# Where the quads stand in a two-layer encoder: one fewer in layer A's output projection, three more in layer B

## The chip, the cores and the metric

The kernel runs on one core of one Trainium2 chip. A core has a matrix engine (TensorE, PE in the profile, with its weight loads as PEld), a vector engine (VectorE, DVE), a scalar engine (ScalarE, ACT), GpSimd (POOL) and a queue engine (SyncE, SP), each with its own instruction stream in a fixed order; semaphores tie the streams together. The metric is the device time of one execution in microseconds. Each version is timed in several runs, and one further execution is profiled.

## The reference

The input x has 256 rows (frames) of 2048 values, all in float32. Two layers and a last norm:

```python
# layer A (chunked attention, 32 heads of 128, chunks of 64 frames)
h = rms_norm(x, a_norm)
q, k, v, g = jnp.split(h @ a_w_in, 4, axis=-1)          # 2048 -> 4 x 4096
o = chunked_relbias_attention(q, k, v, a_rel_bias)
x = x + (o * silu(g)) @ a_w_out                          # 4096 -> 2048
# shared keys and values, and the forget gate
h_kv = rms_norm(x, kv_norm)
k_s, v_s = jnp.split(h_kv @ kv_w, 2, axis=-1)            # 2048 -> 2 x 4096
logf = log_sigmoid(h_kv @ f_w + f_b);  cum = cumsum(logf)
# layer B (forgetting attention: logits q.k/sqrt(128) + cum[t] - cum[s], causal)
q, g = jnp.split(rms_norm(x, b_norm) @ b_w_in, 2, axis=-1)   # 2048 -> 2 x 4096
o = forgetting_attention(q, k_s, v_s, cum)
x = x + (o * silu(g)) @ b_w_out                          # 4096 -> 2048
return rms_norm(x, final_norm)
```

Nearly all of the arithmetic is in the four projections, whose weights are read once.

## The kernel before, in words

**Products.** The weights stay float32 in memory. Each weight tile (`raw`) is split into a high part (`hi`, rounded, made by ScalarE, L243 or L248) and a low part (`lo`, the rest, made by VectorE, L244 or L249); the activations are split the same way once (`xT`, `oA`, `x1T`, `oB`, each with an h and an l). A product is three matmuls, high by high, low by high, high by low, of 128x128 against 128x512 (L185). A *unit* is 512 output columns for all 256 rows (two accumulators); an *entry* is a block of two k-rows (256 input features) of one unit: 2 x 2 x 3 = 12 matmuls. Splits are kept in four buffers each (`SPLIT`), raw tiles in six (`RAW`), so ScalarE and VectorE can run at most four entries ahead of TensorE.

**Quads.** For a pair of units, block b of both may be done together by Winograd's scheme with 7 instead of 8 block products (class `Quad`): 21 matmuls in place of 24. For it VectorE forms four sums of weights (L300, L301, L311, L312) and four low parts (L308), ScalarE the high parts (L306), and the left side needs sums of its own per block (`sum_up`, L393 to L401: five additions, a high part on ScalarE at L400, a low part at L401). Some of the seven products go into sums `p1`, `p5`, `p6`, `p7` that several quads share; after the last quad of a pair they are combined (L351 to L355) and added to what the units give (`add_combined`, L831, or `add_whole`).

**Stages.** Sixteen groups of two heads in layer A (`aqk`, `avg` units, two quads per pair from group 1 on), the output projection of layer A (units `ao0` to `ao3`, 16 entries each), sixteen groups in layer B (`bqg`, `bkv` units, one quad per pair from group 1 on), the output projection of layer B (`bo0` to `bo3`). The forget gate is worked out in group 0 of layer B, in pieces (`forget`, with `zp`, `fps`, the chain on `f_work`, `cp`, `cT`), one piece at a time between the entries of `bkv0` as `FORGET_STEPS` says.

**The attention of a group** is a generator whose steps are woven between the projection's entries. Its steps: split the turned q and k (`wide`, `q`); the scores (`s1p`, `s0p`, L552 and L576) and the softmax; the weights and the gate are turned (`turn`): VectorE transposes in 32x32 blocks (`sgY`, L522), and sixteen transfers, eight each from GpSimd and SP, carry the blocks to their places (`sgZ`, L525); split the turned weights (`wide`, L544 on ScalarE and L545 on VectorE); the product with v (`op`, L552 to L554 and L616); and the gated result goes into the next projection's left side (`oT`, L620, then `oAh`/`oAl` or `oBh`/`oBl`). The output projection therefore needs its last k-rows (entry 15) only after the last attention.

**Order.** `project` (L482) runs an output projection through a list of entries and quads, `Quads.order` makes it: `lead` entries, a quad, three entries, a quad, and so on. After each item the side generators advance by a table of counts: `[4, 1, 0, 1, 5, 1, 1]` means the first step after the fourth item, the next after one more, and so on. The sums of the quads (`open`) have such a table too. The splits are issued four entries ahead. On each engine the instructions run in the order in which the program issues them.

## Time and profile before

| | |
|---|---|
| median of 3 runs | 1736.14 us (1734.17 to 1737.35) |
| profiled execution | 1732.83 us, its span 1731.1 us |
| TensorE busy | 1710.2 us, 99% of the span |
| VectorE busy | 1561.4 us, 90% |
| ScalarE busy | 1195.1 us, 69% |
| GpSimd busy | 301.0 us, 17% |
| DMA, mean | 229 GB/s |

Layer A's groups run to about 690 us, its output projection to about 862, layer B's groups to about 1560, and its output projection to the end. In lines of the profile a number behind L is the line of the kernel before, names are those of the program without buffer numbers, `x` gives the count, a pair of numbers in front of a timeline's row is start and duration, and the brackets at its end give the idle time of the engine before it and what ended it. A matmul's duration is that of its passage through a pipeline; the distance of two starts is what it costs.

### The profile page before, as it was taken

The numbers are of one execution on the slowest core, as the hardware profiler recorded it, in microseconds if no ns is written. First come the engines' busy times: TensorE is split into PE (matmuls) and PEld (weight loads), VectorE is DVE, ScalarE is ACT, GpSimd is POOL, SyncE is SP. The second block draws the span as 40 slices with busy tenths as digits, with TensorE's granted clock in tenths as the row PEclk, the third lists the DMA queues.
The fourth block names the chain that finished last, engine by engine and source line by source line (L and its number), as shares of the span: only waits on it lengthen the run. The fifth ranks groups of instructions, "written<-read, shape, count | busy, mean of one in ns | idle before, by whom it ended". The sixth has DMA issues, their size and how long they took to land.

```text
span 1731.1 us, 26983 instructions
## 1 busy us (share of the span) xinstructions
PE 1710.2 (99%) x8213; PEld 1498.4 (87%) x8213; DVE 1561.4 (90%) x2378; ACT 1195.1 (69%) x2115; POOL 301.0 (17%) x623
## 2 busy tenths in 40 slices
PE   9999999999999999899999999999999999999997
PEld 7888888888888888788888888888888888888886
DVE  8799998999999999888978999999999989996887
ACT  7666666666666666555658788778788878775554
POOL 1011111111111111103102222222222222221000
PEclk9999999999999999999999999999999999999999
DMA  8666666776666666566766666666666666667654
GB/s 309 210 228 245 232 233 206 237 240 235 233 225 231 228 237 231 196 232 225 269 217 219 222 234 231 225 232 229 227 231 232 226 226 229 251 233 251 221 195 146
DMA packets 150320, 396.44 MB, mean 229 GB/s; under 512 B 31104, under 2 KB 51872, under 8 KB 150048
## 3 DMA queue, kind: packets, MB, share of 16 engines
q1 hardware_dynamic: 131536, 373.16, 61.7%
q0 software_dynamic: 17920, 20.48, 4.5%
q8 instruction: 66, 1.08, 0.3%
q10 hardware_dynamic: 720, 1.07, 0.2%
q14 instruction: 78, 0.64, 0.1%
HBM read 351.05 MB, written 4.23 MB: 205 GB/s over the span
## 4 chain that ended last, share of the span: by engine, by line
PE 93%; DVE 3%; DMA 1%; ACT 1%; issue 1%; POOL 0%; SPq 0%; ACTq 0%; DVEq 0%
PE bkv_acc L185 17%; PE bqg_acc L185 17%; PE avg_acc L185 14%; PE aqk_acc L185 13%; PE bo_acc L185 8%; PE ao_acc L185 6%; PE p L553 3%; PE p L554 3%; PE p L552 3%; PE op L616 1%; PE aqk_acc L553 1%; PE s0p L576 1%; PE aqk_acc L554 1%; PE aqk_acc L552 1%; DVE quad_lo L308 1%
## 5 line engine op out<-in xcount | busy, mean ns | idle before, releaser
L525 POOL DMA_DIRECT2D sums<-first x256 | 126.1, 500 | 549.8 <-DVE oT L620 262.5
L243 ACT ACTIVATE bqg_hi<-bqg_raw,gain 128x512 fp32r<-128x512 f32 x226 | 149.5, 713 | 85.6 <-issue 24.9
L244 DVE SCALAR_TENSOR_TENSOR bkv_lo<-bkv_raw,gain,bkv_hi 128x512 fp32r<-128x512 f32 x226 | 161.3, 760 | 17.1 <-ACT bkv_hi L243 16.8
L185 PE MATMUL bkv_acc<-bkv_hi,x1Th 128*128 128x512 f32 x452 | 167.5, 382 | 0.0
L185 PE MATMUL bqg_acc<-bqg_hi,x1Th 128*128 128x512 f32 x452 | 167.4, 382 | 0.0
L185 PE MATMUL bqg_acc<-bqg_lo,x1Th 128*128 128x512 f32 x452 | 166.1, 379 | 0.0
L185 PE MATMUL bkv_acc<-bkv_hi,x1Tl 128*128 128x512 f32 x452 | 166.1, 379 | 0.0
L185 PE MATMUL bkv_acc<-bkv_lo,x1Th 128*128 128x512 f32 x452 | 166.1, 379 | 0.0
L185 PE MATMUL bqg_acc<-bqg_hi,x1Tl 128*128 128x512 f32 x452 | 166.1, 379 | 0.0
L243 ACT ACTIVATE bkv_hi<-bkv_raw,gain 128x512 fp32r<-128x512 f32 x226 | 145.1, 711 | 22.4 <-issue 16.0
L244 DVE SCALAR_TENSOR_TENSOR bqg_lo<-bqg_raw,gain,bqg_hi 128x512 fp32r<-128x512 f32 x226 | 156.2, 741 | 4.6 <-ACT bqg_hi L243 4.5
L525 POOL DMA_DIRECT2D sgZ<-sgY x256 | 125.7, 499 | 156.2 <-PE avg_acc L185 66.7
L185 PE MATMUL aqk_acc<-aqk_hi,xTh 128*128 128x512 f32 x392 | 146.5, 387 | 0.1
L185 PE MATMUL aqk_acc<-aqk_lo,xTh 128*128 128x512 f32 x392 | 143.7, 380 | 1.1 <-DVE aqk_lo L249 1.0
L185 PE MATMUL avg_acc<-avg_hi,xTh 128*128 128x512 f32 x392 | 143.4, 379 | 0.0
L185 PE MATMUL avg_acc<-avg_hi,xTl 128*128 128x512 f32 x392 | 143.4, 379 | 0.0
L185 PE MATMUL avg_acc<-avg_lo,xTh 128*128 128x512 f32 x392 | 143.3, 379 | 0.0
L185 PE MATMUL aqk_acc<-aqk_hi,xTl 128*128 128x512 f32 x392 | 143.3, 379 | 0.0
L249 DVE TENSOR_TENSOR avg_lo<-avg_raw,avg_hi 128x1024 fp32r<-128x1024 f32 x97 | 116.1, 1222 | 16.5 <-ACT avg_hi L248 15.8
L248 ACT ACTIVATE aqk_hi<-aqk_raw 128x1024 fp32r<-128x1024 f32 x95 | 99.9, 1052 | 41.1 <-PE avg_acc L185 15.3
L248 ACT ACTIVATE avg_hi<-avg_raw 128x1024 fp32r<-128x1024 f32 x97 | 100.6, 1052 | 30.8 <-issue 18.1
L249 DVE TENSOR_TENSOR aqk_lo<-aqk_raw,aqk_hi 128x1024 fp32r<-128x1024 f32 x95 | 114.2, 1215 | 5.6 <-ACT aqk_hi L248 5.6
(373 smaller groups left out, 4595.8 us busy)
## 6 DMA issues: line engine op xcount, KB each, us to landing
bqg_raw<-in_b_w_in SPq DMA_DIRECT2D x128, 512.0 KB, 5.1
bkv_raw<-in_kv_w SPq DMA_DIRECT2D x128, 512.0 KB, 4.8
avg_raw<-in_a_w_in SPq DMA_DIRECT2D x127, 512.0 KB, 4.3
aqk_raw<-in_a_w_in SPq DMA_DIRECT2D x125, 512.0 KB, 5.3
ao_raw<-in_a_w_out SPq DMA_DIRECT2D x64, 512.0 KB, 4.7
bo_raw<-in_b_w_out SPq DMA_DIRECT2D x64, 512.0 KB, 4.4
sgZ<-sgY SPq DMA_DIRECT2D x256, 40.0 KB, 2.1
sgZ<-sgY POOLq DMA_DIRECT2D x256, 40.0 KB, 1.9
```

The lines of the kernel that those rows point to most:

```text
L185: pe.matmul(acc[t], x[:, t * P:(t + 1) * P], w, start=t not in begun, stop=last and i == 2)
L243: self.by_act = act.activation(hi[:, j], raw[:, j], AF.Copy, scale=gk)
L244: self.by_dve = dve.scalar_tensor_tensor(lo[:, j], raw[:, j], gk, r32(hi[:, j]), op0=OP.mult, op1=OP.subtract)
L248: self.by_act = act.activation(hi[:, j], raw[:, j], AF.Copy)
L249: self.by_dve = dve.tensor_sub(lo[:, j], raw[:, j], r32(hi[:, j]))
L308: feed.by_dve = dve.tensor_sub(lo[:, :n], src, r32(hi[:, :n]))
L525: queues[j].dma_start(out=r32(z)[j * SQ:(j + 1) * SQ, i], in_=y[i * SQ:(i + 1) * SQ, j])
L552: pe.matmul(out_, a[0], b[0], start=start, stop=False)
L553: pe.matmul(out_, a[0], b[1], start=False, stop=False)
L554: pe.matmul(out_, a[1], b[0], start=False, stop=stop)
L576: pe.matmul(s0p[:, i], q0[:, i], qkT[:, HG + i, 0], start=True, stop=True)
L616: pe.matmul(op[:, i, 1::NT], v1[:, i * DH:(i + 1) * DH], pT[:, i, NT], start=False, stop=i == HG - 1)
```

## The change

It moves quads and steps. Three things:

1. In layer A's output projection the first pair (`ao0`, `ao1`) has two quads instead of three, behind 17 entries instead of 14. The sums of its quads are opened after 8, 11, 30, 34 and 39 items instead of 3, 4, 5, 7 and 33. The steps of the last layer-A attention come one entry later each.
2. Group 0 of layer B has a quad for block 7, as the other groups have: `bqg0` and `bkv0` run seven blocks and a quad stands behind the third entry of `bkv0`. The sums of block 7 are made earlier (`sums_b`), and the pieces of the forget gate stand after entries 0, 1, 4 and 5 of `bkv0` instead of 0, 2, 6 and 7.
3. In layer B's output projection the first pair (`bo0`, `bo1`), which had plain entries alone, has two quads behind 17 entries. The sums are opened after 6, 10, 30, 34 and 39 items instead of 20, 22, 24, 26 and 28. In the last layer-B attention `wide` is split one item sooner (after 15), and `op` and `oT` come two items sooner (after 16 and 17).

In all the program has six matmuls fewer (7991 against 7997 rows on TensorE, 2049 against 2016 on VectorE). Lines of the changed kernel lie three to five lower.

```diff
--- before.py
+++ after.py
@@ -52,7 +52,7 @@
 TERMS = 8
 QUADS = 5
 HEAT = 9
-WAIT = 8
+WAIT = 5
 
 QUADS_A = (1, 2)
 QUADS_B = (2,)
@@ -61,7 +61,7 @@
 B1_STEPS = {3: 1, 5: 1, 6: 2}
 B2_STEPS = {1: 1}
 OLD_B_STEPS = {0: 1, 2: 99}
-FORGET_STEPS = {0: 1, 2: 1, 6: 1, 7: 1}
+FORGET_STEPS = {0: 1, 1: 1, 4: 1, 5: 1}
 
 
 def r32(ap):
@@ -360,10 +360,10 @@
         def __init__(self, name):
             self.name, self.sums = name, {}
 
-        def order(self, first, second, n, lead):
+        def order(self, first, second, n, lead, wait=3):
 
             a, b = ([(sp_, i) for i in range(n, sp_["nk"] // KB)] for sp_ in (first, second))
-            normal = a[:-1] + b[:3] + a[-1:] + b[3:]
+            normal = a[:-1] + b[:wait] + a[-1:] + b[wait:]
             out = normal[:lead]
             for i in range(n):
                 out.append((None, Quad(self, (first, second), i, not i, i == n - 1)))
@@ -430,17 +430,14 @@
     a_pairs = [paired(qkvg[2 * g:2 * g + 2], QUADS_A) for g in range(1, NG)]
     ao = [spec(f"ao{u}", a_w_out[u], KI) for u in range(4)]
     ao_quads, bo_quads = Quads("ao"), Quads("bo")
-    ao_order = ao_quads.order(ao[0], ao[1], 3, 14) + ao_quads.order(ao[2], ao[3], QUADS, 4)
+    ao_order = ao_quads.order(ao[0], ao[1], 2, 17) + ao_quads.order(ao[2], ao[3], QUADS, 4)
     todo += ao_order
     for g in range(NG):
-        qkvg.append(spec(f"bqg{g}", b_w_in[g], KD, g0=GB, quads=len(QUADS_B) * (g > 0)))
-        qkvg.append(spec(f"bkv{g}", kv_w[g], KD, g0=GKV, quads=len(QUADS_B) * (g > 0)))
+        qkvg.append(spec(f"bqg{g}", b_w_in[g], KD, g0=GB, quads=len(QUADS_B)))
+        qkvg.append(spec(f"bkv{g}", kv_w[g], KD, g0=GKV, quads=len(QUADS_B)))
     bo = [spec(f"bo{u}", b_w_out[u], KI, LATE if u == 3 else 0, KEPT if u == 3 else 0) for u in range(4)]
-    todo += whole(qkvg[2 * NG]) + whole(qkvg[2 * NG + 1])
-    b_pairs = [paired(qkvg[2 * g:2 * g + 2], QUADS_B) for g in range(NG + 1, 2 * NG)]
-    bo_order = whole(bo[0]) + whole(bo[1])
-    bo_order.insert(KI // KB + WAIT, bo_order.pop(KI // KB - 1))
-    bo_order += bo_quads.order(bo[2], bo[3], QUADS, 4)
+    b_pairs = [paired(qkvg[2 * g:2 * g + 2], QUADS_B) for g in range(NG, 2 * NG)]
+    bo_order = bo_quads.order(bo[0], bo[1], 2, 17, WAIT) + bo_quads.order(bo[2], bo[3], QUADS, 4)
     todo += bo_order
     feed = Feed(todo)
     order = iter(qkvg)
@@ -854,7 +851,7 @@
                            accum_out=ssq1[:, t, u:u + 1])
         return more and (more, [8, 7, 1, 1, 1] if u % 2 else [11, 1, 1, 1])
 
-    project(oA, ao, ao_order, ao_begun, ao_closed, [(prev, [4, 1, 0, 1, 5, 1, 1]), (ao_quads.open(oA, QUADS), [3, 1, 1, 2, 26])])
+    project(oA, ao, ao_order, ao_begun, ao_closed, [(prev, [5, 1, 0, 1, 5, 1, 1]), (ao_quads.open(oA, QUADS), [8, 3, 19, 4, 5])])
     tot1 = const.tile([P, NT], F32, name="tot1")
     dve.tensor_reduce(tot1, ssq1, axis=AX.X, op=OP.add)
     rsB, halfB = rstd_of(tot1, "b")
@@ -949,17 +946,13 @@
 
         qk, gs = accs["q"]
         kv = accs["kv"]
-        if g:
-            for t in range(NT):
-                whole_ = a_quads.comb[:, NT + t]
-                dve.scalar_tensor_tensor(qk[:, t, GC:], kv[t][:, :GC], rsB[:, t:t + 1], whole_[:, :GC],
-                                         op0=OP.mult, op1=OP.add)
-            for t in range(NT):
-                whole_ = a_quads.comb[:, NT + t]
-                dve.tensor_add(whole_[:, GC:], kv[t][:, GC:], whole_[:, GC:])
-            kv = [a_quads.comb[:, NT + t] for t in range(NT)]
-        else:
-            evac_scaled(kv, 0, GC, rsB, qk[:, :, GC:])
+        whole_ = [a_quads.comb[:, NT + t] for t in range(NT)]
+        for t in range(NT):
+            dve.scalar_tensor_tensor(qk[:, t, GC:], kv[t][:, :GC], rsB[:, t:t + 1], whole_[t][:, :GC],
+                                     op0=OP.mult, op1=OP.add)
+        for t in range(NT):
+            dve.tensor_add(whole_[t][:, GC:], kv[t][:, GC:], whole_[t][:, GC:])
+        kv = whole_
         rest_of = attention(g, biases, qk, lambda: (v, gs), halfB, oB, HALVES, ("last", "last"), home)
         next(rest_of)
         yield
@@ -967,8 +960,8 @@
         yield
         yield from rest_of
 
-    def open_b(accs, g):
-        qk, qg = rows(UN, "qk"), add_whole(accs["qg"], 0) if g else accs["qg"]
+    def open_b(accs):
+        qk, qg = rows(UN, "qk"), add_whole(accs["qg"], 0)
         evac_scaled(qg, 0, GC, rsB, qk[:, :, :GC])
         accs["q"] = qk, gate_from(qg, GC, halfB)
 
@@ -976,22 +969,24 @@
     fg = forget()
     for g in range(NG):
         accs = {}
+        first, second = (Unit(x1T, next(order)) for _ in range(2))
+
+        def sums_b():
+            finish(last[0])
+            a_quads.sum_up(x1T, KD // KB - 1, sums[:, 0], a_quads.comb)
+
+        def products():
+            b_pairs[g][0].step(x1T, first, second)
+            open_b(accs)
+            for t in range(NT):
+                k = a_quads.comb[:, NT + t, :GC]
+                act.activation(k, k, AF.Copy, scale=rsB[:, t:t + 1])
+
         if g:
-            first, second = (Unit(x1T, next(order)) for _ in range(2))
             accs["qg"] = drive(rest(first), prev, B1_STEPS, {}, old, OLD_B_STEPS)
-
-            def products():
-                b_pairs[g - 1][0].step(x1T, first, second)
-                open_b(accs, g)
-                for t in range(NT):
-                    k = a_quads.comb[:, NT + t, :GC]
-                    act.activation(k, k, AF.Copy, scale=rsB[:, t:t + 1])
-
-            accs["kv"] = drive(rest(second), prev, B2_STEPS, {QUADS_B[0]: products})
         else:
-            accs["qg"] = drive(unit(x1T), last[0], {2: 99})
-            accs["kv"] = drive(unit(x1T), fg, FORGET_STEPS, {2: lambda: open_b(accs, g)})
-            a_quads.sum_up(x1T, KD // KB - 1, sums[:, 0], a_quads.comb)
+            accs["qg"] = drive(rest(first), None, {}, {2: sums_b})
+        accs["kv"] = drive(rest(second), prev if g else fg, B2_STEPS if g else FORGET_STEPS, {QUADS_B[0]: products})
         old, prev = prev, side_b(g, accs)
         advance(prev)
 
@@ -1033,11 +1028,11 @@
     def bo_begun(u, left):
         if left == (4 if u else 1):
             load_xin(x1d, u)
-        if left == 2 and u == 3:
+        if left == 2 and u % 2:
             add_combined(bo_quads, u)
 
     def bo_closed(u, acc):
-        if u == 2:
+        if u % 2 == 0:
             add_combined(bo_quads, u)
         xin = xins.pop(u)
         for t in range(NT):
@@ -1047,8 +1042,8 @@
             if u == 3:
                 finish_tile(t)
 
-    project(oB, bo, bo_order, bo_begun, bo_closed, [(old, [1, 2, 0]), (prev, [4, 2, 1, 1, 1, 7, 2, 1]),
-                                                 (bo_quads.open(oB, QUADS), [20, 2, 2, 2, 2])])
+    project(oB, bo, bo_order, bo_begun, bo_closed, [(old, [1, 2, 0]), (prev, [4, 2, 1, 1, 1, 6, 1, 1]),
+                                                 (bo_quads.open(oB, QUADS), [6, 4, 20, 4, 5])])
 
 
 _INS = ["x", "x_t", "gains", "a_w_in", "a_rel_bias", "a_w_out", "kv_w", "f_w", "f_b", "b_w_in", "b_w_out",
```

Three places show what moves. In the rows, the number at the end of a name tells one buffer from another.

**VectorE in layer A's output projection, up to the transpose `sgY` of the last attention.** L249 is the low part of an entry, L393 to L401 are sums of a quad's left side, `csc` scales the softmax. Before:

```order
L396 TENSOR_TENSOR ao_quad_7189<-ao_quad_7189 128x128
L397 TENSOR_TENSOR ao_quad_7189<-ao_quad_7189 128x128
L398 TENSOR_TENSOR ao_quad_7189<-ao_quad_7189 128x128
L249 TENSOR_TENSOR ao0_lo12_7330<-ao0_raw12_7139,ao0_hi12_7329 128x1024
L399 TENSOR_TENSOR ao_quad_7189<-ao_quad_7189 128x128
L598 RECIPROCAL csc_7303<-sm_7265 128x4
L249 TENSOR_TENSOR ao0_lo13_7353<-ao0_raw13_7157,ao0_hi13_7352 128x1024
L401 TENSOR_TENSOR ao_sums2_7275<-ao_quad_7189,ao_sums2_7275 128x512
L599 TENSOR_TENSOR csc_7303<-csc_7303,half_a_395 128x4
L393 TENSOR_TENSOR ao_quad_7189<-oAh0_184,oAl0_188 128x512
L249 TENSOR_TENSOR ao0_lo14_7371<-ao0_raw14_7175,ao0_hi14_7370 128x1024
L522 STREAM_TRANSPOSE sgY_7310<-sg_7263 128x1280
```

The changed kernel, from the scores (`sg`) on:

```order
L586 SCALAR_TENSOR_TENSOR sg_7265<-s0p_7256,tb_7017 128x2x128
L587 TENSOR_REDUCE nm_7266<-sg_7265 128x2 x2
L249 TENSOR_TENSOR ao0_lo11_7278<-ao0_raw11_7139,ao0_hi11_7277 128x1024
L595 RECIPROCAL csc_7295<-sm_7267 128x4
L596 TENSOR_TENSOR csc_7295<-csc_7295,half_a_395 128x4
L249 TENSOR_TENSOR ao0_lo12_7322<-ao0_raw12_7157,ao0_hi12_7321 128x1024
L393 TENSOR_TENSOR ao_quad_7339<-oAh0_184,oAl0_188 128x512
L519 STREAM_TRANSPOSE sgY_7302<-sg_7265 128x1280
```

Of the sums that stood between the scores and the transpose one addition (L393) is left ahead of it; the rest now stands behind it.

**VectorE in layer B's output projection, from the transpose of the last attention to the split of `wide`.** Before:

```order
L249 TENSOR_TENSOR bo0_lo11_16429<-bo0_raw11_16270,bo0_hi11_16428 128x1024
L522 STREAM_TRANSPOSE sgY_16453<-sg_16398 128x1280
L249 TENSOR_TENSOR bo0_lo12_16473<-bo0_raw12_16302,bo0_hi12_16472 128x1024
L249 TENSOR_TENSOR bo0_lo13_16491<-bo0_raw13_16326,bo0_hi13_16490 128x1024
L249 TENSOR_TENSOR bo0_lo14_16509<-bo0_raw14_16344,bo0_hi14_16508 128x1024
L249 TENSOR_TENSOR bo1_lo0_16527<-bo1_raw0_16374,bo1_hi0_16526 128x1024
L249 TENSOR_TENSOR bo1_lo1_16545<-bo1_raw1_16410,bo1_hi1_16544 128x1024
L249 TENSOR_TENSOR bo1_lo2_16563<-bo1_raw2_16432,bo1_hi2_16562 128x1024
L249 TENSOR_TENSOR bo1_lo3_16585<-bo1_raw3_16476,bo1_hi3_16584 128x1024
L545 TENSOR_TENSOR wide_16602<-sgZ_16454,wide_16602 128x2x128 x2
```

The changed kernel, first around the transpose and then around `wide`:

```order
L249 TENSOR_TENSOR bo0_lo14_16499<-bo0_raw14_16317,bo0_hi14_16498 128x1024
L393 TENSOR_TENSOR bo_quad_16385<-oBh0_8665,oBl0_8669 128x512
L519 STREAM_TRANSPOSE sgY_16479<-sg_16422 128x1280
L396 TENSOR_TENSOR bo_quad_16385<-bo_quad_16385 128x128
L397 TENSOR_TENSOR bo_quad_16385<-bo_quad_16385 128x128
L398 TENSOR_TENSOR bo_quad_16385<-bo_quad_16385 128x128
L249 TENSOR_TENSOR bo1_lo2_16522<-bo1_raw2_16341,bo1_hi2_16521 128x1024
L399 TENSOR_TENSOR bo_quad_16385<-bo_quad_16385 128x128
```

```order
L249 TENSOR_TENSOR bo1_lo5_16578<-bo1_raw5_16434,bo1_hi5_16577 128x1024
L300 TENSOR_TENSOR bo_quad_16385<-bo1_raw0_16458,bo0_raw0_16456 128x512
L301 TENSOR_TENSOR bo_quad_16385<-bo1_raw0_16458 128x512
L308 TENSOR_TENSOR quad_lo0_16600<-bo0_raw0_16456,quad_hi0_16599 128x1024
L542 TENSOR_TENSOR wide_16617<-sgZ_16480,wide_16617 128x2x128
L311 TENSOR_TENSOR bo0_raw0_16456<-bo1_raw0_16458,bo_quad_16385 128x512
L542 TENSOR_TENSOR wide_16617<-sgZ_16480,wide_16617 128x2x128
L312 TENSOR_TENSOR bo0_raw0_16456<-bo0_raw0_16456 128x512
L308 TENSOR_TENSOR quad_lo1_16623<-bo_quad_16385,quad_hi1_16622 128x1024
```

The transpose has the thirteenth entry's low part and one addition ahead of it that stood behind it or were not there; `wide` stands two entries sooner, and the first sums and the first low part of a quad stand ahead of it.

**VectorE in group 0 of layer B, at the forget gate.** L894 to L910 before (L891 to L907 after) are the gate's chain, L244 the low part of an entry, L308 that of a quad. Before:

```order
L894 COPY f_work_8962<-fps_8959 128x64
L895 TENSOR_TENSOR f_work_8962<-f_work_8962,fps_8959 128x64
L244 SCALAR_TENSOR_TENSOR bkv0_lo6_8994<-bkv0_raw6_8808,gain_83,bkv0_hi6_8993 128x512
L897 SCALAR_TENSOR_TENSOR f_work_8962<-f_work_8962,rstd_b_8660,fb_8670 128x32 x2
L244 SCALAR_TENSOR_TENSOR bkv0_lo6_8994<-bkv0_raw6_8808,gain_83,bkv0_hi6_8993 128x512
L899 SCALAR_TENSOR_TENSOR f_work_8962<-f_work_8962 128x64
L901 TENSOR_SCALAR f_work_8962<-f_work_8962 128x64
L909 TENSOR_SCALAR f_work_8962<-f_work_8962 128x64
L902 RECIPROCAL f_work_8962<-f_work_8962 128x64
L244 SCALAR_TENSOR_TENSOR bkv0_lo7_9014<-bkv0_raw7_8828,gain_83,bkv0_hi7_9013 128x512
L903 TENSOR_TENSOR f_work_8962<-f_work_8962 128x64
L244 SCALAR_TENSOR_TENSOR bkv0_lo7_9014<-bkv0_raw7_8828,gain_83,bkv0_hi7_9013 128x512
```

The changed kernel:

```order
L308 TENSOR_TENSOR quad_lo2_8944<-bkv0_raw7_8705,quad_hi2_8943 128x512
L894 SCALAR_TENSOR_TENSOR f_work_8920<-f_work_8920,rstd_b_8651,fb_8661 128x32 x2
L896 SCALAR_TENSOR_TENSOR f_work_8920<-f_work_8920 128x64
L898 TENSOR_SCALAR f_work_8920<-f_work_8920 128x64
L906 TENSOR_SCALAR f_work_8920<-f_work_8920 128x64
L899 RECIPROCAL f_work_8920<-f_work_8920 128x64
L900 TENSOR_TENSOR f_work_8920<-f_work_8920 128x64
L901 TENSOR_TENSOR f_work_8920<-f_work_8920 128x64
L902 TENSOR_SCALAR f_work_8920<-f_work_8920 128x64
L904 SCALAR_TENSOR_TENSOR f_work_8920<-f_work_8920 128x64 x2
L308 TENSOR_TENSOR quad_lo3_8966<-bqg0_raw7_8703,quad_hi3_8965 128x1024
L904 SCALAR_TENSOR_TENSOR f_work_8920<-f_work_8920 128x64
```

The chain now runs between the third and the fourth low part of the quad, and `bkv0`'s next entries stand behind it; the low parts of plain entries that were woven into it come later.

## The prediction

> **What bounds the kernel now.** I read the page first: its busy line, its chain of waits and the group of the main matmul.
>
> ```profile
> PE 1710.2 (99%) x8213; PEld 1498.4 (87%) x8213; DVE 1561.4 (90%) x2378; ACT 1195.1 (69%) x2115; POOL 301.0 (17%) x623
> PE 93%; DVE 3%; DMA 1%; ACT 1%; issue 1%; POOL 0%; SPq 0%; ACTq 0%; DVEq 0%
> L185 PE MATMUL bkv_acc<-bkv_hi,x1Th 128*128 128x512 f32 x452 | 167.5, 382 | 0.0
> ```
>
> TensorE is busy for 99% of the span and is 93% of the chain, so time can be won in two ways only: fewer matmuls, or fewer holes between them. The 382 ns of a matmul is its length in a pipeline, not its price. The price is read from the chain in order of time, of which a piece gives start, length and count:
>
> ```profile
> 1014.89 7.77 PE bkv_acc L185 x36
> ```
>
> 7.77/36 = 0.216 us per 512-column matmul. An entry (two k-rows of one unit, 12 matmuls) is 2.59 us, a quad (21 matmuls in place of 24) 4.53 us.
>
> The holes are in the list of what TensorE waited for (total, times, longest):
>
> ```profile
> PE op L552 <- ACT wide L544: 4.2, 1, 4.2
> PE aqk_acc L553 <- DVE quad_lo L308: 1.7, 3, 0.8
> PE s1p L552 <- ACT q L544: 1.0, 2, 0.6
> PE p L553 <- DVE quad_lo L308: 0.6, 1, 0.6
> ```
>
> These four are the longest, 7.5 us together, and one hole is 4.2 of it. The windows around it (length, TensorE busy, granted clock, DMA share) and the timeline show where it is: in layer A's output projection, at `op` of the last layer-A attention.
>
> ```profile
> 690.00:724.90 34.90, 33.95 (x162) 1.00 0.63 208
> 729.30:732.80 3.50, 3.45 (x14) 0.56 0.76 284
> ...
> 703.15 0.38 PE L185 MATMUL ao_acc<-ao_hi,oAl 128*128 128x512 f32 x1
> 703.98 0.38 PE L552 MATMUL s1p<-wide,q 128*128 128x256 f32 x1 [0.45 <-ACT q L544]
> 704.99 0.37 PE L554 MATMUL s1p<-wide,q 128*128 128x256 f32 x1
> 705.85 0.57 PE L576 MATMUL s0p<-sums,q 128*128 128x128 f32 x3 [0.50 <-DMA ao_raw<-in_a_w_out]
> ...
> 724.72 0.38 PE L185 MATMUL ao_acc<-ao_lo,oAh 128*128 128x512 f32 x1
> 729.35 0.58 PE L552 MATMUL op<-wide,vh 128*128 128x256 f32 x1 [4.25 <-ACT wide L544]
> 732.36 0.47 PE L185 MATMUL ao_acc<-ao_lo,oAh 128*128 128x512 f32 x1
> ```
>
> Three losses. s1p begins at 703.98 instead of 703.15 + 0.22 = 703.37, and s0p at 705.85 instead of 704.99 + 0.11: 0.61 + 0.75 = 1.36 us. `op` begins at 729.35 instead of 724.94: 4.41 us. After that the granted clock is 0.56 for 3.5 us: 3.5 x 0.44 = 1.55 us. Together 7.32 us.
>
> Why `op` is late is read backwards:
>
> ```profile
> 728.88 0.72 ACT L544 ACTIVATE wide<-sgZ 128x256 fp32r<-128x256 f32 x2 [5.12 <-DMA sgZ<-sgY]
> ...
> 720.29 6.08 SPq L525 DMA_DIRECT2D sgZ<-sgY  x8
> ...
> 718.72 1.51 DVE L522 STREAM_TRANSPOSE sgY<-sg 128x1280 f32<-128x1280 f32 x1
> ```
>
> ScalarE stood 5.12 us for the transfers of the turned tile; SP takes 6.08 us to issue its eight, from the moment the transpose on VectorE ends (718.72 + 1.51 = 720.23). From there to `wide` is 8.65 us. And the transpose waits in VectorE's own order, behind the sums of the quads:
>
> ```profile
> L393 DVE TENSOR_TENSOR ao_quad<-oAh,oAl x5: 677/682/685, 699.0 to 790.7; 128x512 f32<-128x512 f32 x5
> L396 DVE TENSOR_TENSOR ao_quad<-ao_quad x5: 251/285/293, 699.7 to 791.4; 128x128 f32<-128x128 f32 x5
> L401 DVE TENSOR_TENSOR ao_sums<-ao_quad,ao_sums x5: 684/685/692, 706.2 to 794.2; 128x512 fp32r<-128x512 f32 x5
> ```
>
> One set of sums is 0.68 + 4 x 0.285 + 0.685 = 2.5 us.
>
> **The change part by part.** *Matmuls.* Layer A's first pair loses a quad (+3 matmuls), layer B's group 0 gains one (-3), layer B's first pair gains two (-6): 6 fewer, 6 x 0.216 = **-1.30 us**.
>
> *Layer A's last attention.* Each step comes one entry later. Without the 1.36 us, s0p lies at 705.85 - 1.36 + 2.59 = 707.08. `op` stood behind twelve entries and two matmuls of the next; now it stands behind thirteen entries. TensorE reaches it at 724.94 - 1.36 + 2.59 - 2 x 0.216 = 725.74. From s0p to the transpose was 718.72 - 705.85 = 12.87 us; in it lay three L401, eight of L396 to L399 and two L393, 3 x 0.685 + 8 x 0.285 + 2 x 0.682 = 5.7 us. In the new order one L393 is left there. So the transpose starts near 707.08 + 12.87 - 5.0 = 714.95 and ends near 716.5; with the same 8.65 us, `wide` starts at 725.1, 0.6 us ahead of TensorE. Its low part on VectorE (0.76 us for both in layer B's row below) and the second set's L400, which now stands on ScalarE between the two halves of `wide`, make `op`'s later matmuls wait a little. I take 0.6 us of lateness; the bounds are 0 (the transfers land sooner, as below) and 2.0 (they need the 10 us of layer B, below). The clock then stays full: the two gaps of 0.45 and 0.50 us lie in the window with clock 1.00. Gain 7.32 - 0.6 = **-6.7 us**.
>
> On the clock the Trainium skill, "TensorE: Matmul & The Clock Gate", section "Why this matters for your kernels", says that gaps beyond some 3 us bring the half clock back. The trace agrees at 4.25 us; by that rule the remaining 0.6 costs 0.6, while by rows alone the limit lies anywhere between 0.50 and 4.25 us.
>
> *Layer B's group 0.* The quad's work on VectorE is four half-size sums and four low parts, with their prices from the other groups; behind them stand the low part of a plain block, the addition of combined products, and three windows with VectorE's busy time:
>
> ```profile
> L300 DVE TENSOR_TENSOR first<-bkv_raw,bqg_raw x15: 691/692/693, 928.4 to 1532.1; 128x512 f32<-128x512 f32 x15
> L308 DVE TENSOR_TENSOR quad_lo<-bqg_raw,quad_hi x30: 1216/1222/1227, 931.5 to 1541.5; 128x1024 fp32r<-128x1024 f32 x30
> L308 DVE TENSOR_TENSOR quad_lo<-bkv_raw,quad_hi x15: 647/651/814, 936.7 to 1540.4; 128x512 fp32r<-128x512 f32 x15
> L244 DVE SCALAR_TENSOR_TENSOR bqg_lo<-bqg_raw,gain,bqg_hi 128x512 fp32r<-128x512 f32 x226 | 156.2, 741 | 4.6 <-ACT bqg_hi L243 4.5
> L831 DVE TENSOR_TENSOR xin<-xin,bo_quad x2: 1217/1218/1218, 1709.4 to 1710.5; 128x1024 f32<-128x1024 f32 x2
> ...
> 870.00:910.00 40.00, 30.71 (x72) 1.00 0.61 205
> 1600.00:1652.00 52.00, 42.16 (x65) 1.00 0.60 204
> 1652.00:1704.00 52.00, 45.71 (x49) 1.00 0.66 221
> ```
>
> 4 x 0.69 + 3 x 1.22 + 0.65 = 7.1 us, less 3.0 us for the low parts of the two blocks that it replaces (four L244), into a stretch where VectorE has 40 - 30.71 = 9.3 us idle. It fits as a sum. But the last low part (quad_lo3) now stands behind the forget gate's chain of small operations, which TensorE releases only with `fps`; I place both its end and its need within half a microsecond of each other. Bounds: 0, and two waits like the longest known on a quad's low part, 2 x 0.8 = 1.6 us. I take **+0.7**.
>
> *Layer B's output projection, first pair.* `op` comes two entries sooner, so I ask whether its data do:
>
> ```profile
> 1603.90 0.27 PE L552 MATMUL op<-wide,vh 128*128 128x256 f32 x1
> ...
> 1581.77 1.51 DVE L522 STREAM_TRANSPOSE sgY<-sg 128x1280 f32<-128x1280 f32 x1
> ...
> 1597.30 0.71 ACT L544 ACTIVATE wide<-sgZ 128x256 fp32r<-128x256 f32 x2
> 1598.56 0.76 DVE L545 TENSOR_TENSOR wide<-sgZ,wide 128x256 fp32r<-128x256 f32 x2
> ...
> L525 POOL DMA_DIRECT2D sgZ<-sgY x8: 496/498/498, 1583.8 to 1589.1; - x8
> DMA to landing us min/median/max: 1.7/1.9/4.6
> ```
>
> TensorE comes to `op` at 1603.90 - 5.18 = 1598.7. The last transfer was issued at 1589.1 and took at most 4.6 us: landed by 1593.7, 10.4 us after the transpose's end. With one more low part (1.22) and one L393 (0.68) ahead of it, at most 1.9 us, the transpose slips to 1583.7, the landing to 1595.6, and `wide` is done by 1596.4. Its low part now stands behind the first quad's sums and low part and is done near 1597.5. Slack 1.2 us, so **0**, with 1.5 us as the upper bound. VectorE between 1600 and 1652 trades three sets of sums (-7.5) and four low parts (-4.9) for two quads (+14.2) and two additions of combined products (+2.4), 42.16 + 4.2 = 46.4 of 52 us.
>
> *Sums among the quads.* In both second pairs sets of sums now stand between quads, two more in layer A and three more in layer B. An interval is 4.53 + 3 x 2.59 = 12.3 us of TensorE against 4 x 0.68 + 3 x 1.22 + 0.69 + 3 x 1.22 = 10.7 us of VectorE; with sums 13.2. Five such intervals, each 0.9 us over: 0 (the splits that lie ready absorb it) to 4.5; I take **+0.8**, since VectorE keeps 6 us of idle time in 1652 to 1704.
>
> Sum: -1.30 - 6.7 + 0.7 + 0 + 0.8 = **-6.5 us**. The profiled execution took 1732.83 us (span 1731.1 and 1.7 around it), so its counterpart is 1726.3. The median of the runs is 1736.14, 3.3 us above the profiled one; I take the same difference there: **1729.6 us**.
>
> **The rivals.**
>
> *The op of layer A stays late (0.09).* The transfers, not the transpose, set the time. For it: in layer A they landed slowly.
>
> ```profile
> L525 SPq DMA_DIRECT2D sgZ<-sgY x8: 508/586/592, 720.3 to 725.9; - x8
> DMA to landing us min/median/max: 2.9/4.8/5.7
> ```
>
> 4.8 us at the median against 1.9 in layer B. Against it: the issue follows the transpose at once (720.23, 720.29). If from the transpose's end to `wide` it takes 12.5 us or more, the hole is beyond 3 us again and the clock falls; what is then left of the gain, with the hole as before, is -1.30 - 1.36 + 1.5 = -1.2: 1734.9. The Trainium skill, "DMA: Bandwidth & Descriptors", section "Queues, rings and completion order", says that each engine takes descriptors in ring order, so that the turned tile's would stand behind the 512 KB weight loads that SP issued just before; the slower landing above agrees.
>
> *VectorE becomes the bound (0.16).* The three risks come at their upper bounds: 1.6 + 1.5 + 4.5 = 7.6 instead of 1.5 us. For it: 90% busy, and the waits on quad_lo in the list. Against it: those waits are 1.7 + 0.6 = 2.3 us in 58 quads. -1.30 - 6.7 + 7.6 = -0.4: 1735.7.
>
> *Slower (0.07).* The sums among the quads are not hidden at all: VectorE's idle time in the second pairs cannot be used, because it is time in which it waits for ScalarE's high parts or for a free buffer. Two more sets in layer A's second pair and three in layer B's, 5 x 2.5 = 12.5 us, then lie on TensorE's path: -1.30 - 6.7 + 0.7 + 12.5 = +5.2, 1741.3. It decides once more than 10.8 of these 12.5 us show (-7.3 + 10.8 = 3.5). For it: 45.71 of 52 us are busy there already, and 5 of the 7.5 us would fall into the 6.3 that are left. Against it: the one set that stands there in the kernel before, begun at 790.7 (the last start in L393's row), left in 737 to 870 no wait of TensorE above 0.2 us:
>
> ```profile
> PE ao_acc L185 <- ACT ao_hi L248: 0.2, 1, 0.2
> ```
>
> **How the numbers follow.** The forecast has 0.68. About 0.2%, 3.5 us, is what a measurement of this kernel can tell from no change; the forecast lies beyond it, the first two rivals within (0.25), the third above (0.07). The range: with all three risks at 0 and `op` in time it is -1.30 - 7.32 = -8.6, 1727.5, less 2 us for the spread of single runs (1734.17 to 1737.35): 1725.5. Upwards it takes in both rivals that end within 0.2%: 1736.0.
>
> **What would show it.** No wait of `op` on `wide` above 1 us in layer A, the transpose of sgY ending by 717 and no window there with a clock below 1; six matmuls fewer; no new wait above 1 us at quad_lo3 of layer B's group 0 or at layer B's `op`. I am wrong if the hole at `op` is still over 3 us, or if waits on quad_lo grow from 2.3 to over 6 us.

## The result and the profile after

| | before | after |
|---|---|---|
| median (4 runs each) | 1735.16 us (1733.26 to 1737.35) | 1725.16 us (1723.84 to 1727.88) |
| profiled execution, span | 1732.83, 1731.1 us | 1723.84, 1722.1 us |

The ratio is 0.9945, 95% interval 0.9933 to 0.9957: faster by 10.0 us at the median, by 9.0 us in the spans. The prediction said faster by 6.5 us. The median lies 0.3 us below the lower end of its range. That range was reckoned from a median of 1736.14 us before; the ratio applied to that gives 1726.6, which lies inside.

The busy line of the page after, in the order PE, PEld, DVE, ACT, POOL (busy us, share, instructions):

```profile
PE 1705.8 (99%) x8207; PEld 1496.4 (87%) x8207; DVE 1577.2 (92%) x2404; ACT 1200.3 (70%) x2123; POOL 300.3 (17%) x623
```

Six matmuls fewer, as forecast, and VectorE 16 us busier. TensorE's waits after (total, times, longest):

```profile
PE aqk_acc L550 <- DVE quad_lo L308: 1.9, 3, 0.8
PE p L550 <- DVE quad_lo L308: 1.5, 1, 1.5
PE heat L111 <- DVE zeros L108: 1.3, 1, 1.3
...
PE op L613 <- DMA sums<-first: 0.4, 1, 0.4
PE op L550 <- DVE wide L542: 0.3, 1, 0.3
```

The wait of `op` on ScalarE's `wide`, 4.2 us before, is not in the list. One wait has grown: that of `p` on a quad's low part, from 0.6 to 1.5 us. The windows of the changed kernel (length, TensorE busy, clock, DMA share, GB/s):

```profile
690.00:737.00 47.00, 47.00 (x230) 1.00 0.68 229
737.00:870.00 133.00, 132.78 (x620) 1.00 0.74 245
870.00:910.00 40.00, 40.00 (x206) 1.00 0.59 194
1600.00:1652.00 52.00, 52.00 (x242) 1.00 0.69 233
1652.00:1704.00 52.00, 50.40 (x233) 1.00 0.57 190
```

In the kernel before, the first of these windows was

```profile
690.00:737.00 47.00, 41.80 (x196) 0.96 0.58 194
```

TensorE was busy for 41.80 of 47 us, with half the clock in a part of it; now it is busy throughout at full clock.

To see where the 9.0 us came from I took, for each pair of neighbouring matmuls, the distance of their starts less what it is in an undisturbed stream (0.216 us for 512 columns, 0.111 for 256, 0.092 for 128), and added up this *delay* by stretch (in places of the kernel before, us):

| stretch | before | after | difference |
|---|---|---|---|
| start and layer A's groups, to 640 | 12.05 | 11.62 | -0.43 |
| first pair of layer A's output projection up to its first quad (737), with the hole | 8.25 | 0.38 | -7.87 |
| the first pair's quads and the second pair | 1.13 | 0.59 | -0.54 |
| group 0 of layer B | 1.16 | 1.21 | +0.05 |
| groups 1 to 15 of layer B | 3.47 | 3.62 | +0.15 |
| first pair of layer B's output projection | 0.22 | 0.20 | -0.02 |
| its second pair and the end | 1.21 | 2.12 | +0.91 |
| sum | 27.49 | 19.74 | -7.75 |

With the six matmuls (-1.30) that is -9.05, the difference of the spans. The stretch with the hole is nearly the whole story; the rest is small change of both signs. Below, the delay of the first pair is that of the second row, the delay of the second pair that of the third.

The same chain at `op` after the change, from timelines of four engines (start, duration):

```profile
706.19 0.61 PE L573 MATMUL s0p<-sums,q 128*128 128x128 f32 x4
...
712.76 1.50 DVE L519 STREAM_TRANSPOSE sgY<-sg 128x1280 f32<-128x1280 f32 x1
...
714.34 5.00 SPq L522 DMA_DIRECT2D sgZ<-sgY  x8
...
720.87 0.42 ACT L541 ACTIVATE wide<-sgZ 128x256 fp32r<-128x256 f32 x1
...
724.77 0.27 PE L549 MATMUL op<-wide,vh 128*128 128x256 f32 x1
```

No row has an idle time in brackets. From s0p to the transpose it is 6.57 us (12.87 before), from the transpose's end to `wide` 6.61 us (8.65 before), and `op` comes 3.9 us after `wide` has begun.

### The profile page after: what moved, and what is told of

It is laid out like the page before. It is cut to its first block, busy times and chain, and to the rows that moved or that the text cites. A ratio compares the mean times of both kernels' runs of the same rounds, so it can differ in the third digit from the quotient of the medians.

```text
span 1722.1 us, 27009 instructions
## 1 busy us (share of the span) xinstructions
PE 1705.8 (99%) x8207; PEld 1496.4 (87%) x8207; DVE 1577.2 (92%) x2404; ACT 1200.3 (70%) x2123; POOL 300.3 (17%) x623
## 4 chain that ended last, share of the span: by engine, by line
PE 79%; DVE 2%; DMA 1%; ACT 1%; issue 1%; ACTq 0%; SPq 0%; DVEq 0%
PE bqg_acc L185 16%; PE bkv_acc L185 16%; PE avg_acc L185 9%; PE aqk_acc L185 8%; PE bo_acc L185 7%; PE ao_acc L185 7%; PE p L550 2%; PE p L549 2%; PE p L551 2%; PE op L613 1%; PE s0p L573 1%; PE aqk_acc L550 1%; PE aqk_acc L551 0%; PE aqk_acc L549 0%; DVE quad_lo L308 0%
## 5 line engine op out<-in xcount | busy, mean ns | idle before, releaser
L244 DVE SCALAR_TENSOR_TENSOR bkv_lo<-bkv_raw,gain,bkv_hi 128x512 fp32r<-128x512 f32 x224 | 160.5, 761 | 14.9 <-ACT bkv_hi L243 14.6
L244 DVE SCALAR_TENSOR_TENSOR bqg_lo<-bqg_raw,gain,bqg_hi 128x512 fp32r<-128x512 f32 x224 | 154.9, 743 | 2.8 <-ACT bqg_hi L243 2.8
L249 DVE TENSOR_TENSOR avg_lo<-avg_raw,avg_hi 128x1024 fp32r<-128x1024 f32 x97 | 116.1, 1222 | 15.9 <-ACT avg_hi L248 15.3
L249 DVE TENSOR_TENSOR aqk_lo<-aqk_raw,aqk_hi 128x1024 fp32r<-128x1024 f32 x95 | 114.5, 1218 | 5.4 <-ACT aqk_hi L248 5.3
```

Of the source, the lines that this page charges most:

```text
L244: self.by_dve = dve.scalar_tensor_tensor(lo[:, j], raw[:, j], gk, r32(hi[:, j]), op0=OP.mult, op1=OP.subtract)
L249: self.by_dve = dve.tensor_sub(lo[:, j], raw[:, j], r32(hi[:, j]))
```

## The experiments

### Which part gives what

Each part alone on the kernel before. Layer A's output projection:

```diff
-    ao_order = ao_quads.order(ao[0], ao[1], 3, 14) + ...
+    ao_order = ao_quads.order(ao[0], ao[1], 2, 17) + ...
-    project(oA, ao, ..., [(prev, [4, 1, 0, 1, 5, 1, 1]), (ao_quads.open(oA, QUADS), [3, 1, 1, 2, 26])])
+    project(oA, ao, ..., [(prev, [5, 1, 0, 1, 5, 1, 1]), (ao_quads.open(oA, QUADS), [8, 3, 19, 4, 5])])
```

> The kernel before with the change in layer A's output projection alone (two quads behind 17 entries, sums opened later, attention steps one entry later). It has three matmuls more than before, +0.65 us. If the parts of the change act each for itself, all of the 7.9 us at the hole and the 0.5 us of the second pair come with it: -7.8 us against before, ratio 0.9955. If part of the gain needs the moves in layer B (earlier end of the quads, other DMA traffic), it is smaller, -6 us or less.

Measured: ratio 0.9953 (0.9940 to 0.9965), -8.2 us. The delay of the first pair is 0.38 and of the second 0.59, the very values of the whole change: this part needs nothing from layer B.

The quad of group 0 of layer B alone (the second item of the change, the rest as before):

> The kernel before with the quad in group 0 of layer B alone. Three matmuls fewer, -0.65 us. If VectorE's extra work there is hidden, as the changed kernel's trace suggests, -0.6 us against before; by the prediction's price of the late low part, 0 us; by its upper bound, +1 us. The hole in layer A's output projection stays as in the kernel before.

Measured: 0.9996 (0.9988 to 1.0005). That is -0.7 us with an uncertainty of 1.5, no difference that can be told. In its trace the delay of group 0 is 1.56 against 1.16 us, in the whole change 1.21. The 0.4 us lie at `cT`, where TensorE waits for the end of the forget gate's chain (`cum`); for the quad's low part, which the prediction feared, TensorE did not wait.

Layer B's output projection alone (the third item):

> The kernel before with the change in layer B's output projection alone. Six matmuls fewer, -1.30 us; the wait on the quads' low part near the end grows by what the changed kernel's trace shows (0 to +0.9 us): -0.4 to -1.3 us against before. If op, two entries sooner, comes ahead of its data, a wait of op on wide appears; I expect none.

Measured: 1.0004 (0.9996 to 1.0013), no gain that can be told. No wait of `op` on `wide` is there in layer B; but TensorE's wait near the end is:

```profile
PE op L550 <- ACT wide L542: 4.2, 1, 4.2
PE p L551 <- DVE quad_lo L308: 1.7, 1, 1.7
```

The first row is layer A's hole, which this kernel keeps. The second is the new cost. The delay of the end is 2.36 against 1.21 us: of the 1.30 us of six matmuls 1.15 are given back. The sum of the three parts' ratios, -0.47%, -0.04% and +0.04%, is -0.47%, against -0.55% for the whole; the intervals do not tell these apart.

### What makes the hole: sums, steps or transfers

Three theories: the sums of the quads stand ahead of the transpose on VectorE (order); the steps of the attention come too early in the projection (steps); the turned tile's transfers are slow, because the quads' weights are loaded at that time (transfers). First only the sums' places, on the kernel before:

```diff
-    ... (ao_quads.open(oA, QUADS), [3, 1, 1, 2, 26])
+    ... (ao_quads.open(oA, QUADS), [8, 3, 3, 16, 3])
```

> The kernel before with nothing changed but the places of the sums in layer A's output projection (8, 11, 14, 30, 33 items instead of 3, 4, 5, 7, 33). Theory of the order: the hole before op is there because the sums stand ahead of the transpose on VectorE; without them the transpose starts near 711.5, op finds its data, the 4.41 us and the 1.55 us of half clock go, the two gaps at s1p and s0p (1.36 us) stay: -6.0 us. Theory of the steps: the hole goes because the attention's steps have an entry more; then nothing changes here, 0 us. Theory of the transfers: the turned tile lands late because of the traffic of the quads' weight loads, which is still the traffic of before: the transfers still take 4.8 us at the median, and at least 3 us of the hole stay.

Measured: 0.9959 (0.9947 to 0.9972), -7.1 us; in the trace the delay of the first pair goes from 8.25 to 2.18, -6.07 us. The hole is gone with no step moved: the places of the sums are enough to make it or to remove it, and the theory of the steps is not needed for it. The theory of the transfers falls as it was put: with the loads of before they landed in 2.6 us at the median instead of 4.8. The two gaps before the scores stay, in the list of TensorE's waits between 600 and 900 us:

```profile
PE s0p L576 <- ACT ao_hi L248: 0.5, 1, 0.5
PE s1p L552 <- ACT q L544: 0.4, 1, 0.4
```

Those two gaps are what the steps are for. The changed kernel with the old steps:

```diff
-    ... (prev, [5, 1, 0, 1, 5, 1, 1])
+    ... (prev, [4, 1, 0, 1, 5, 1, 1])
```

> The changed kernel with the old table of the last layer-A attention's steps (4, 1, 0, 1, 5, 1, 1). Theory of the order: the sums still stand behind the transpose, op finds its data; only the gaps at s1p and s0p come back, since the split's data land at 703.1 whatever the steps: +1.4 us against the changed kernel. Theory of the steps: the hole of 4 us with the half clock comes back, +6 to +7 us.

Measured: 0.9956 (0.9944 to 0.9969), some 1.9 us above the changed kernel by the ratios, which the two intervals do not tell apart; in the trace the delay of the first pair is 2.21 instead of 0.38, +1.8 us, and it lies at s1p and s0p alone. Taken apart in this order, the sums first, the change's 7.9 us are 6.1 us from the places of the sums and 1.8 us from the steps. The order matters: a run below shows that the hole can also go while three sets stay early.

The reverse, the first two sets early again in the changed kernel:

```diff
-    ... (ao_quads.open(oA, QUADS), [8, 3, 19, 4, 5])
+    ... (ao_quads.open(oA, QUADS), [3, 1, 26, 4, 5])
```

> The changed kernel with the first two sums of layer A's output projection opened after 3 and 4 items again (the others stay at 30, 34, 39); steps and quads as changed. Theory of the order: up to two sets of sums (5 us, less what falls into VectorE's idle time before the scores) stand ahead of the transpose again, it starts near 715 to 717 instead of 712.8, and op waits 0.3 to 2.5 us; below 3 us the clock stays full: +0.3 to +2.5 us against the changed kernel. Theory of the steps: 0 us. Theory of the transfers: 0 us, since the traffic is that of the changed kernel.

Measured: 0.9939 (0.9925 to 0.9953), no slower than the change. From s0p to the transpose it is 6.44 us, so two early sets cost nothing there: with the steps an entry later they fit ahead of the scores, and TensorE waits 0.3 us at s0p. `op` did not wait, which is below what the theory of the order expected.

### What one set costs

So I moved one set only, the fourth, on the kernel before:

```diff
-    ... (ao_quads.open(oA, QUADS), [3, 1, 1, 2, 26])
+    ... (ao_quads.open(oA, QUADS), [3, 1, 1, 25, 3])
```

> The kernel before with one set of sums moved in layer A's output projection: the fourth is opened after 30 items instead of 7 (3, 4, 5, 30, 33). Theory of the order: one of the sets between the scores and the transpose is gone, the transpose comes 2.4 us sooner, op waits 0.2 to 2.0 us instead of 4.25, and since that is below 3 us the clock stays full: -4 to -5.8 us against before, more than the 2.4 us that were moved. Theory of the transfers: they still land slowly behind the weight loads, the hole stays above 3 us, the clock falls: -1 us or less.

Measured: 1.0006 (0.9997 to 1.0015), nothing. The forecast by the order was wrong in its price. That by the transfers has the right number, but the run does not speak for it, since the transpose hardly moved. The chain in this kernel:

```profile
707.83 0.68 PE L576 MATMUL s0p<-sums,q 128*128 128x128 f32 x4 [0.47 <-DMA ao_raw<-in_a_w_out]
...
720.42 1.51 DVE L522 STREAM_TRANSPOSE sgY<-sg 128x1280 f32<-128x1280 f32 x1 [0.21 <-ACT sg L603]
...
722.00 6.74 SPq L525 DMA_DIRECT2D sgZ<-sgY  x8
...
731.31 0.72 ACT L544 ACTIVATE wide<-sgZ 128x256 fp32r<-128x256 f32 x2 [6.11 <-DMA sgZ<-sgY]
...
731.78 0.58 PE L552 MATMUL op<-wide,vh 128*128 128x256 f32 x1 [4.70 <-ACT wide L544]
```

From s0p to the transpose it is 12.59 us instead of 12.87. Of the fourth set only its first addition (0.68 us) stood ahead of the transpose; the others already stood behind, as the order in the part on the change shows. I had counted a whole set. From the transpose's end (721.93) to `wide` it is 9.38 us, against 8.65; in the two runs with a part of layer B alone, whose code is that of the kernel before up to here, it is 8.98 and 8.54, so a good part of this difference may be chance. The landing of the sixteen transfers (the time from the issue of one to its data's arrival) in this kernel and in two others, in the order this kernel, the next one, the changed kernel:

```profile
DMA to landing us min/median/max: 2.9/5.6/6.4
```

```profile
DMA to landing us min/median/max: 2.4/3.1/3.8
```

```profile
DMA to landing us min/median/max: 1.8/2.0/2.3
```

Next the third set, and with it the fourth, since they go in order:

```diff
-    ... (ao_quads.open(oA, QUADS), [3, 1, 1, 2, 26])
+    ... (ao_quads.open(oA, QUADS), [3, 1, 10, 16, 3])
```

> The kernel before with the third set of sums opened after 14 items instead of 5, and with it, since they go in order, the fourth after 30 (3, 4, 14, 30, 33); the first two stay where they are. Moving the fourth alone gained nothing. Theory that it is the third set, which lies ahead of the softmax's scale (csc) on VectorE: the transpose comes 5 to 6 us sooner, its transfers are issued before the weight loads of the quads pile up and land in 2 to 3 us instead of 5, op finds its data, -6 us against before. Theory that each set costs its own 2.5 us: the second still stands ahead of the transpose, the transpose comes 2.4 to 5 us sooner, a hole of 0 to 2 us stays, the clock is full: -4 to -6 us. Theory that the transfers alone make the hole: they land in 5 us still, -1 us.

Measured: 0.9980 (0.9972 to 0.9989), -3.5 us; in the trace the delay of the first pair is 3.40 (-4.85), that of the next row of the table 2.13 (+1.0, all of it at the first quad, from 739.8 to 741.9 us). Its chain:

```profile
709.82 0.68 PE L576 MATMUL s0p<-sums,q 128*128 128x128 f32 x4 [0.47 <-DMA ao_raw<-in_a_w_out]
...
719.41 1.51 DVE L522 STREAM_TRANSPOSE sgY<-sg 128x1280 f32<-128x1280 f32 x1
...
728.06 0.72 ACT L544 ACTIVATE wide<-sgZ 128x256 fp32r<-128x256 f32 x2 [3.46 <-DMA sgZ<-sgY]
...
728.53 0.38 PE L552 MATMUL op<-wide,vh 128*128 128x256 f32 x1
```

From s0p to the transpose 9.59 us: with the third set gone from it the way is 3.0 us shorter (12.59 to 9.59). With the first two moved too (the run with all sums late) it is 6.76, 2.8 us shorter again. The price of 2.5 us for a set is not what makes these numbers: it adds up lengths that overlap. From start to start an L393 takes 0.60 us in the kernel before, each of L396 to L399 0.20 and an L401 0.61, together 2.0. The rest is that fewer low parts of entries (L249, 1.13 us from start to start) stand between the scores and the transpose: five with the fourth set moved, four here, two with all sums late.

The hole itself is gone already here, since `wide` comes in time once the transpose is earlier and the transfers take 7.14 instead of 9.38 us. So each theory had a part: by sets, the shift of the transpose; by the third set, that `op` finds its data, though the transpose came 3 and not 5 to 6 us sooner.

The other way round, the third set back in the changed kernel:

```diff
-    ... (ao_quads.open(oA, QUADS), [8, 3, 19, 4, 5])
+    ... (ao_quads.open(oA, QUADS), [3, 1, 1, 25, 4])
```

> The changed kernel with the third set of sums back after 5 items (3, 4, 5, 30, 34), the other way round of the run above, with the steps an entry later and two quads. Theory of the third set: the transpose comes 1 to 3 us later than in the changed kernel, which has some 2 us to spare at op: 0 to +1 us, with the full clock. Theory that each set costs 2.5 us: three sets stand ahead of the transpose, 5 us or more later, a hole of 3 us and the half clock: +4 to +6 us.

Measured: 0.9951 (0.9937 to 0.9965), within the noise of the changed kernel (0.9945). From s0p to the transpose 8.75 us, 2.2 more than in the changed kernel; the delay of the first pair is 1.34 instead of 0.38, +1.0 us, with no hole. Only the third set costs something, as its theory said; the first two are done ahead of the scores.

This run also answers the one with the fourth set moved. Both open the first four sets after 3, 4, 5 and 30 items, but here the steps come an entry later and the pair has two quads; there the way from s0p to the transpose is 12.59 us and `op` waits 4.70, here 8.75 and no hole. So the later steps with two quads remove the hole as well, since VectorE then does two of the sets before the scores. Either move is enough to end the hole. What counts is what stands between the scores and the transpose, and the 6.1 and 1.8 us above hold only for the sums moved first. No run moved the steps alone. Side by side (us):

| kernel | s0p to transpose | transpose's end to `wide` | landing, median | `op` waits |
|---|---|---|---|---|
| fourth set moved | 12.59 | 9.38 | 5.6 | 4.70 |
| before | 12.87 | 8.65 | 4.8 | 4.25 |
| third and fourth moved | 9.59 | 7.14 | 3.1 | under 0.5 |
| changed, third set back | 8.75 | 7.32 | 3.3 | under 0.5 |
| all sums late | 6.76 | 6.82 | 2.6 | none |
| changed | 6.57 | 6.61 | 2.0 | none |

The kernels with a late transpose have the slow transfers, so there the sums seem to cost twice, once in VectorE's order and once more in the transfers. That the loads ahead of the transfers are the reason fits the sequence on SP. In the kernel before, four loads of 512 KB (three weight tiles and a residual tile, `xin`) are issued in the 5.3 us ahead of sgZ:

```profile
715.01 1.73 SPq L207 DMA_DIRECT2D ao_raw<-in_a_w_out  x2
716.79 0.43 SPq L828 DMA_DIRECT2D xin<-in_x  x1
718.83 0.33 SPq L207 DMA_DIRECT2D ao_raw<-in_a_w_out  x1
720.29 6.08 SPq L525 DMA_DIRECT2D sgZ<-sgY  x8
```

and in the changed kernel the last load was issued by 712.6, 1.7 us ahead of the first sgZ:

```profile
709.63 2.97 SPq L207 DMA_DIRECT2D ao_raw<-in_a_w_out  x2
714.34 5.00 SPq L522 DMA_DIRECT2D sgZ<-sgY  x8
```

All thirteen profiles follow this: with four such loads in the 5.3 us ahead of sgZ (four profiles) the sixteen landed in 4.8 to 5.6 us at the median, with three (two profiles) in 3.1 and 3.3, with two (seven) in 2.0 to 2.6. Their place behind the loads in SP's queue is not all of it, since the eight that GpSimd issues on a queue of its own landed as late: 4.8 us at the median against SP's 5.0 in the kernel before, 1.9 against 2.1 after. No run changed the loads alone, so this reason is argued, not shown.

### How much room VectorE has

Three quads instead of two in both first pairs of the changed kernel:

```diff
-    ao_quads.order(ao[0], ao[1], 2, 17)       ... [8, 3, 19, 4, 5]
+    ao_quads.order(ao[0], ao[1], 3, 17)       ... [8, 3, 6, 13, 4]
-    bo_quads.order(bo[0], bo[1], 2, 17, WAIT) ... [6, 4, 20, 4, 5]
+    bo_quads.order(bo[0], bo[1], 3, 17, WAIT) ... [6, 4, 7, 13, 4]
```

> The changed kernel with three quads instead of two in the first pair of both output projections, behind 17 entries, the third set of sums opened after 17 items (8, 11, 17, 30, 34 and 6, 10, 17, 30, 34). Six matmuls fewer, -1.30 us against the changed kernel, if VectorE has room for it (it is busy for some 85 to 90% there); if not, the wait on quads' low parts grows and takes it back: 0 to +1 us.

Measured: 0.9977 (0.9967 to 0.9988), some 5.5 us slower than the change by the ratios, in spite of six matmuls fewer. TensorE's new waits from 737 us on:

```profile
PE bo_acc L185 <- DVE xin L1000: 1.5, 1, 1.5
PE ao_acc L185 <- DVE xin L841: 1.5, 1, 1.5
PE ao_acc L550 <- DVE quad_lo L308: 1.3, 3, 0.8
...
PE bo_acc L549 <- ACT quad_hi L306: 0.7, 1, 0.7
PE p L550 <- DVE quad_lo L308: 0.7, 1, 0.7
```

VectorE is late with the residual (`xin`, L841 and L1000), which must empty an accumulator before the next pair can begin, and with low parts after it. Ahead of L841 stands the addition of the pair's combined products, which are complete only after the third quad:

```profile
772.79 2.35 DVE L828 TENSOR_TENSOR xin<-xin,ao_quad 128x1024 f32<-128x1024 f32 x2
775.07 1.28 DVE L841 TENSOR_TENSOR xin<-ao_acc,xin 128x512 f32<-128x512 f32 x2
```

This is near the rival in which VectorE becomes the bound, but VectorE was busy for 34.44 of the 39 us from 737 to 776 there. By these rows it is late by its order; whether its total would allow a third quad in another order was not tried.

### The wait that grew

The wait near the end grew in the changed kernel. The last three sets of sums of layer B's output projection sooner:

```diff
-    ... (bo_quads.open(oB, QUADS), [6, 4, 20, 4, 5])
+    ... (bo_quads.open(oB, QUADS), [6, 4, 18, 3, 3])
```

> The changed kernel with the last three sets of sums of layer B's output projection opened after 28, 31 and 34 items instead of 30, 34 and 39. If the fifth set, which stands ahead of the third quad's sums of weights, is what makes the wait on the low part near the end grow (from 0.74 to 1.63 us of delay), it falls back to 0.7 to 0.8 us: -0.9 us against the changed kernel. If that wait grows because weight tiles come later for another reason (six matmuls fewer ahead of them), it stays: 0 us. Sets that crowd the first quad of the second pair could cost up to 1 us there.

Measured: 0.9962 (0.9949 to 0.9975), some 2.9 us slower than the change by the ratios, at the edge of what the intervals can tell apart; its trace shows 1.4 us more delay in this stretch. The delay at that place is 1.40 us, where the changed kernel has 1.63 and the kernel before 0.74, and 1.4 us are lost at the first quad of the second pair. So the fifth set is not the reason, or not alone. What the low part stands behind in VectorE's order is a split whose weight tile comes late; in the changed kernel ScalarE waits for it:

```profile
1675.75 1.06 ACT L248 ACTIVATE bo_keep<-bo_raw 128x1024 fp32r<-128x1024 f32 x1 [3.66 <-DMA bo_raw<-in_b_w_out]
```

In the kernel before the same wait is 2.75 us. The delay was 0.95 to 1.89 us in the six profiled kernels with two quads in layer B's first pair, 0.52 to 0.86 in the six with none. Since the same code there gave 0.95, 1.40, 1.63 and 1.68 us in four kernels that differ only in layer A, a good part of it varies from execution to execution. Why the tile lands later stays open.

## Why the prediction was right, and where it was not

**What bounds the kernel: right.** The hole at `op` with its half clock and the two gaps were 7.3 us by the rows; the stretch gave 7.87 us.

**Matmuls, -1.30: right**, 8213 to 8207.

**Layer A's last attention, -6.7: right in kind, too small.** Two steps of it failed, in the same direction. The transpose was put at 714.95 and came at 712.76: 0.9 us because s0p came at 706.19 instead of 707.08, and 1.3 us because the way from s0p was 6.57 instead of 7.9 us. (Of the 0.9 us 0.4 are no merit of the change: the whole projection began at 689.9 instead of 690.3.) That the way came near its forecast is in part luck. The 5.0 us that were taken off for the sums add up lengths that overlap; from start to start they are 4.0. Not in the sum was that three low parts of entries (L249, 1.13 us each) left the stretch with them, five before and two after, while VectorE now waits there for ScalarE for 1.0 us: 4.0 + 3.4 - 1.0 = 6.4, close to the measured 12.87 - 6.57 = 6.3. And the transfers were taken with the 8.65 us of before, although part of that was their own lateness: 6.61 us. So the 0.6 us that I took for `op`'s lateness is 0: the high parts of `wide` were done 2.6 us ahead of `op`, the low parts 1.1 us.

**Layer B's group 0, +0.7: too large.** In the changed kernel TensorE's list shows no wait between 860 and 960 us. The quad's low part was done at 887.5, ahead of its need. What showed with this part alone, 0.4 us, was at `cT`.

**Layer B's `op`, 0: right.** Its rows after the change:

```profile
1575.14 1.50 DVE L519 STREAM_TRANSPOSE sgY<-sg 128x1280 f32<-128x1280 f32 x1
...
1587.56 0.72 ACT L541 ACTIVATE wide<-sgZ 128x256 fp32r<-128x256 f32 x2 [1.36 <-DMA sgZ<-sgY]
...
1588.96 0.42 DVE L542 TENSOR_TENSOR wide<-sgZ,wide 128x256 fp32r<-128x256 f32 x1
...
1590.07 0.27 PE L549 MATMUL op<-wide,vh 128*128 128x256 f32 x1
```

10.9 us from the transpose's end to `wide`, where 10.4 was taken for the landing, and `wide` done 0.7 us ahead of `op` where 1.2 was forecast. ScalarE waits for the transfers here now, so a later landing would eat into the 0.7 us that are left.

**Sums among the quads, +0.8: right in sum (-0.54 + 0.91 = +0.4), not in reason.** In layer A the second pair became smoother, since the old gaps there (0.40 and 0.41 us of delay) shrank to 0.39. In layer B the loss came at a low part whose split waits for a weight tile, and that wait varies from execution to execution.

**The sum.** The forecast was -6.5 us, the spans give -9.0. Of the difference 1.2 us lie at the hole (-7.87 for -6.7), 0.65 at group 0 of layer B and 0.4 among the quads; 0.3 us come from groups that no version touches. Of the signs named ahead, all came true: `op` of layer A did not wait, the transpose ended at 714.3, and the waits on `quad_lo` grew from 2.3 to 3.6 us, not to over 6.

**The rivals.** That `op` stays late because of its transfers did not come true: it needed 12.5 us or more from the transpose's end to `wide`, and the longest in any run was 9.38, with the transpose late as well. That transfers land slowly in this stretch was right all the same, 4.8 to 5.6 us in four profiles. VectorE as the bound did not come with two quads in a first pair; with three TensorE waited for VectorE, by its order. That sums among the quads are not hidden at all falls: five sets more, 12.5 us by the prediction's price, left +0.4 us.

**The clock.** The prediction could place the limit only between 0.50 and 4.25 us. Gaps of 1.5 us at TensorE in the run with three quads left the granted clock at 1.00, and a hole of 4.70 us took it down:

```profile
774.00:777.00 3.00, 1.52 (x7) 1.00 0.63 246
```

```profile
729.00:733.00 4.00, 1.22 (x4) 0.70 0.77 281
733.00:737.00 4.00, 4.00 (x14) 0.50 0.38 124
```

(first the run with three quads, then that with the fourth set moved). This agrees with the Trainium skill, "TensorE: Matmul & The Clock Gate", section "Why this matters for your kernels", which warns of gaps beyond some 3 us. Three other profiles do not agree: the runs with layer B's output projection alone, with the third and fourth set moved, and with the first two sets early. In a group of layer A that no version touches they show half the clock for 3.4 us with no wait of TensorE above 0.8 us; here the last of them:

```profile
275.00:278.40 3.40, 2.25 (x13) 1.00 0.53 217
278.40:281.80 3.40, 3.40 (x10) 0.50 0.50 158
```

The other ten have similar waits at this place and kept the full clock there. So no limit on a single gap can be read here, and the measurement decides against taking the page's figure as one. What fits all thirteen profiles is the filling of stretches of 3.41 us, counted from the clock's rise at the start. Every fall of the clock before the end begins on this grid and lasts one or two such stretches. In the stretch ahead of each half-clock one, matmuls at their undisturbed price fill at most 38.5%; ahead of all others up to the last matmul they fill 39.8% or more. This was found afterwards, and no run tested it.
